# A tiled softmax: ten loads and thirteen stores of mixed sizes become eight and eight of 16 rows per partition, and the last three groups are scaled by one broadcasting VectorE multiplication each

## The chip, the core and the metric

The kernel runs on one core of one Trainium2 chip. The metric is the device time of one execution in microseconds (us). Five engines of the core appear here: DVE (VectorE), ACT (ScalarE), POOL (GpSimd), SP (SyncE, which only issues transfers) and PE (TensorE, not used). Transfers run on 16 DMA engines. The letter q behind an engine's name (ACTq, SPq) means its instruction queue, which issues DMAs and waits on semaphores.

## The reference

The input x has the shape 16 x 1024 x 512 in float32. The output is the softmax over the last axis:

```python
x_max = np.max(x, axis=-1, keepdims=True)
exp_x = np.exp(x - x_max)
return (exp_x / np.sum(exp_x, axis=-1, keepdims=True)).astype(np.float32)
```

There are 16,384 rows of 512 numbers, 2 KB each. Both the input and the output have 33.55 MB, so 67.1 MB pass through the DMA engines in any version.

## The kernel before

**Chunks.** The rows are cut into chunks. A chunk with R rows per partition has 128 x R rows; partition p holds R neighbouring rows, so each partition's piece of a chunk is one contiguous stretch of R x 2 KB in memory. `CHUNKS` lists R and the place in the on-chip buffer `held`, which has room for 96 rows per partition (`SBUF_ROWS`). Before the change there are ten chunks: of 3, 5 and 8 rows, and then seven of 16. The first eight fill the buffer. The last two reuse places: chunk 8 takes rows 0 to 15, where chunks 0, 1 and 2 were, and chunk 9 takes rows 16 to 31, where chunk 3 was.

**Groups.** The work on a chunk is done in groups of at most `GROUP` = 8 rows (lines 108 to 116), 17 groups in all. For each group there are four steps, all in place in `held`:

- `rowmax` (line 127): one DVE reduction gives the negative maximum of each row, `shift`.
- `exps` (line 135): one ACT activation per row computes exp(x - max) and its sum, `sums`.
- `scale`, first part (line 147): one DVE reciprocal of the sums, `recip`.
- `scale`, second part: the rows are multiplied by `recip`. All groups but the last `ON_VECTOR` = 3 do it on POOL, with one tensor_tensor instruction whose second operand is `recip` broadcast along the row (line 150). The last three do it on DVE, with one tensor_scalar instruction per row (line 157).

**Order.** The order is written by hand: each engine executes its instructions in the order of the loop at lines 173 to 183. For each group it is `rowmax(g)`, `exps(g)`, then `scale` of the group before. At the chunks in `FINISH_BEFORE` the group before is scaled first. So a reciprocal usually stands behind the next group's reduction on DVE, and a store stands behind the next group's activations on ACT.

**Loads** (line 122) are issued on SP's queue. The first `EARLY` = 8 are issued at once, three of them ahead of the barrier that opens the program (`AT_HEAD`). The other two stand behind stores (`AFTER_STORE`): load 8 is issued behind store 2's group and must wait until the stores of the places that it overwrites have landed; load 9 likewise waits for both stores of chunk 3.

**Stores** (line 163) are issued on ACT's queue. Each waits for the multiplication of its rows. `STORE_ROWS` lets chunks 3, 4 and 5 be stored in halves of 8 rows, so there are 13 stores: of 3, 5 and 8 rows, six halves of 8 rows, and four of 16 rows. A partition's piece of a transfer appears in the trace as one packet: 6, 10, 16 or 32 KB.

Of the kernel before, what the change touches and what calls it, by code (L numbers as in the profile page):

```python
# [1 line left out]

# [4 lines left out]

F32 = mybir.dt.float32
EXP = mybir.ActivationFunctionType.Exp
AX = mybir.AxisListType.X  # L10


CHUNKS = [
    (3, 0), (5, 3), (8, 8), (16, 16), (16, 32), (16, 48), (16, 64), (16, 80), (16, 0), (16, 16),
]
SBUF_ROWS = 96

EARLY = 8
AFTER_STORE = {2: [8], 3: [9]}

GROUP = 8

FINISH_BEFORE = (1, 2, 3)

STORE_ROWS = {3: 8, 4: 8, 5: 8}

ON_VECTOR = 3

ON_ACT = ()

AT_HEAD = {mybir.EngineType.SP: 3}

def loads_at_the_head(nc):

    main, body = nc.main_func.blocks[0], nc.main_func.blocks[1]
    for engine, count in AT_HEAD.items():
        loads = [
            i  # L40
            for i in body.instructions
            if i.engine == engine and type(i).__name__ == "InstDMACopy"
        ][:count]
        barrier = next(
            n
            for n, i in enumerate(main.instructions)
            if i.engine == engine and type(i).__name__ == "InstDrain"
        )
        for load in loads:
            body.instructions.remove(load)  # L50
        main.instructions[barrier:barrier] = loads


def one_barrier_on_exit(nc):


    end = nc.main_func.blocks[2].instructions

    def of(engine, kind):
        return [i for i in end if i.engine == engine and type(i).__name__ == kind]  # L60

    for engine in (
        mybir.EngineType.Activation,
        mybir.EngineType.PE,
        mybir.EngineType.DVE,
        mybir.EngineType.SP,
    ):
        arrivals = [i for i in of(engine, "InstDrain") if i.has_update()]
        leaves = of(engine, "InstEventSemaphore")
        assert len(arrivals) == len(leaves) == 2  # L70
        end.remove(leaves[0])
        end.remove(arrivals[1])
    gather, release, gather_2, release_2 = of(mybir.EngineType.Pool, "InstEventSemaphore")
    end.remove(release)
    end.remove(gather_2)

@with_exitstack
def kernel(
    ctx: ExitStack,
    tc: tile.TileContext,  # L80
    x: bass.AP,
    out: bass.AP,
):
    nc = tc.nc
    nc.at_finalize(loads_at_the_head)
    nc.at_finalize(one_barrier_on_exit)
    P = nc.NUM_PARTITIONS

    x_flat = x.flatten_outer_dims()
    out_flat = out.flatten_outer_dims()  # L90
    n, d = x_flat.shape
    assert n == P * sum(R for R, _ in CHUNKS)


    src, dst, at = [], [], 0
    for R, _ in CHUNKS:
        for flat, views in ((x_flat, src), (out_flat, dst)):
            part = flat[at : at + P * R, :]
            views.append(part.rearrange("(p r) d -> p r d", r=R))
        at += P * R  # L100

    data = ctx.enter_context(tc.tile_pool(name="data", bufs=1))
    stats = ctx.enter_context(tc.tile_pool(name="stats", bufs=4))
    held = data.tile([P, SBUF_ROWS, d], F32, name="held")
    place = [held[:, s : s + R, :] for R, s in CHUNKS]


    groups = []
    for k, (R, _) in enumerate(CHUNKS):
        m = -(-R // GROUP)  # L110
        cuts = [R * i // m for i in range(m + 1)]
        since = 0
        for a, b in zip(cuts, cuts[1:]):
            ends = b == R or b - since >= STORE_ROWS.get(k, R)
            groups.append((k, a, b, since if ends else None))
            since = b if ends else since
    shift = [None] * len(groups)
    sums = [None] * len(groups)

    def load(k):  # L120
        queue = nc.scalar if k in ON_ACT else nc.sync
        queue.dma_start(out=place[k], in_=src[k])

    def rowmax(g):
        k, a, b, _ = groups[g]
        shift[g] = stats.tile([P, b - a], F32, name="shift", tag="shift")
        nc.vector.reduce_max(  # L127
            out=shift[g], in_=place[k][:, a:b, :], axis=AX, negate=True
        )

    def exps(g):
        k, a, b, _ = groups[g]
        sums[g] = stats.tile([P, b - a], F32, name="sums", tag="sums")
        for r in range(a, b):
            nc.scalar.activation(  # L135
                out=place[k][:, r, :],
                in_=place[k][:, r, :],
                func=EXP,
                bias=shift[g][:, r - a : r - a + 1],
                scale=1.0,  # L140
                accum_out=sums[g][:, r - a : r - a + 1],
            )

    def scale(g):
        k, a, b, since = groups[g]
        recip = stats.tile([P, b - a], F32, name="recip", tag="recip")
        nc.vector.reciprocal(out=recip, in_=sums[g])  # L147
        on_pool = g < len(groups) - ON_VECTOR
        if on_pool:
            nc.gpsimd.tensor_tensor(  # L150
                out=place[k][:, a:b, :],
                in0=place[k][:, a:b, :],
                in1=recip.unsqueeze(2).to_broadcast([P, b - a, d]),
                op=mybir.AluOpType.mult,
            )
        for r in () if on_pool else range(a, b):
            nc.vector.tensor_scalar_mul(  # L157
                out=place[k][:, r, :],
                in0=place[k][:, r, :],
                scalar1=recip[:, r - a : r - a + 1],  # L160
            )
        if since is not None:
            nc.scalar.dma_start(  # L163
                out=dst[k][:, since:b, :], in_=place[k][:, since:b, :]
            )
        if b == CHUNKS[k][0]:
            for later in AFTER_STORE.get(k, ()):
                load(later)

    with tc.manual_schedule():  # L170
        for k in range(EARLY):
            load(k)
        waiting = None
        for g, (k, a, _, _) in enumerate(groups):
            if waiting is not None and a == 0 and k in FINISH_BEFORE:
                scale(waiting)
                waiting = None
            rowmax(g)
            exps(g)
            if waiting is not None:  # L180
                scale(waiting)
            waiting = g
        scale(waiting)


# [1 line left out]
_INS = ['x']  # L187
_OUTS = [((16, 1024, 512), 'float32')]


# [23 lines left out]
```

## Time and profile before

| what | value |
| --- | --- |
| median of four runs | 161.56 us (161.42 to 161.57) |
| the profiled execution's own time | 161.57 us |
| its span, first to last event of the program | 159.7 us |
| DVE busy | 82.6 us (52%) in 58 instructions |
| ACT busy | 92.9 us (58%) in 257 instructions |
| POOL busy | 91.2 us (57%) in 18 instructions |
| DMA, mean over the span | 67.13 MB, 420 GB/s |

The page divides the span into 40 slices and gives for each the busy tenths of every engine and the mean busy share of the 16 DMA engines. A line per DMA queue says how many packets and bytes it moved and what share of 16 engines' time its packets took: q1 carries SP's loads, q10 carries ACT's stores. The groups list the busy time and the mean duration of each instruction form. The timeline gives single instructions with their start, and in brackets what ended the idle time before them. The chain of waits follows back from the last *instruction*; a DMA that lands after it is not part of it. Beside these views the trace holds one record per DMA packet (queue, start, duration, size), and the prediction uses these too.

### The profile page before, as it was taken

What the parts mean: (1) busy time and instruction counts of PE and PEld (TensorE: products, weight loads), DVE (VectorE), ACT (ScalarE), POOL (GpSimd) and SP (SyncE); (2) the same over time, 40 slices, a digit from 0 to 9 for tenths busy, and PEclk for the clock granted to TensorE, in tenths of its full rate; (3) what the DMA queues carried; (4) which work ended last, traced back from release to release, by engine and by line L of the source; (5) the groups of instructions that cost most, each with busy time, mean ns of one, the idle gap of its engine ahead of it and who ended that gap; (6) DMA issues with size and microseconds to landing.
All of it is one profiled execution on the core that took longest, in us unless ns stands there. A gap on an engine that the chain in (4) does not pass through costs nothing.

```text
span 159.7 us, 442 instructions
## 1 busy us (share of the span) xinstructions
DVE 82.6 (52%) x58; ACT 92.9 (58%) x257; POOL 91.2 (57%) x18
## 2 busy tenths in 40 slices
DVE  0470903980966567393855867387489935000000
ACT  0719076039949796976979957993995760000000
POOL 0060912940899999999999999999930000000000
DMA  7999989999999999999999999989999999999993
GB/s 279 431 455 403 438 367 448 476 397 397 460 414 439 418 427 431 460 410 435 418 480 414 412 435 423 480 369 447 431 435 492 396 427 443 443 410 418 484 402 164
DMA packets 3316, 67.13 MB, mean 420 GB/s; under 512 B 369, under 2 KB 369, under 8 KB 625
## 3 DMA queue, kind: packets, MB, share of 16 engines
q1 hardware_dynamic: 1440, 33.56, 49.5%
q10 hardware_dynamic: 1872, 33.56, 48.9%
q14 instruction: 4, 0.02, 0.0%
HBM read 33.55 MB, written 33.55 MB: 420 GB/s over the span
## 4 chain that ended last, share of the span: by engine, by line
POOL 51%; issue 12%; ACT 11%; DVE 7%; DMA 3%; ACTq 0%; DVEq 0%; POOLq 0%
POOL held L150 51%; ACT held L135 11%; DVE held L157 4%; DMA held<-in_x_dram 3%; DVE shift L127 3%; ACTq L163 0%; DVE recip L147 0%; DVEq L209 0%; POOLq L150 0%; DVEq L147 0%; ACTq L135 0%
## 5 line engine op out<-in xcount | busy, mean ns | idle before, releaser
L135 ACT ACTIVATE held<-held,shift 128x512 f32<-128x512 f32 x128 | 90.4, 708 | 33.0 <-POOL held L150 29.9
L150 POOL TENSOR_TENSOR held<-held,recip 128x4096 f32<-128x4096 f32 (+2 forms) x14 | 91.0, 6526 | 25.8 <-DVE recip L147 25.8
L127 DVE TENSOR_REDUCE shift<-held 128x8 f32<-128x4096 f32 (+2 forms) x17 | 70.3, 4139 | 5.3 <-DMA held<-in_x_dram 5.2
L147 DVE RECIPROCAL recip<-sums 128x8 f32<-128x8 f32 (+2 forms) x17 | 3.4, 200 | 46.0 <-ACT held L135 46.0
L135 ACT ACTIVATION_READ_ACCUMULATOR held<-held,shift 128x1 f32 x128 | 23.9, 187 | 0.0
L157 DVE TENSOR_SCALAR held<-held,recip 128x512 f32<-128x512 f32 x24 | 10.0, 489 | 0.1
L135 ACT ACT_TABLE_LOAD x1 | 1.3, 1283 | 4.5 <-DMA held<-in_x_dram 4.5
L198 POOL MEMSET const-float32-0.0<- 128x1 f32 x1 | 0.1, 98 | 0.2 <-issue 0.2
L198 POOL MEMSET const-bfloat16-1.0<- 128x1 bf16 x1 | 0.1, 101 | 0.0
L198 POOL MEMSET const-uint8-127<- 128x1 uint8 x1 | 0.1, 101 | 0.0
L198 POOL MEMSET const-float32-1.0<- 128x1 f32 x1 | 0.1, 98 | 0.0
## 6 DMA issues: line engine op xcount, KB each, us to landing
held<-in_x_dram SPq DMA_DIRECT2D x7, 4096.0 KB, 39.0
out_dram<-held ACTq DMA_DIRECT2D x4, 4096.0 KB, 29.2
out_dram<-held ACTq DMA_DIRECT2D x7, 2048.0 KB, 38.0
held<-in_x_dram SPq DMA_DIRECT2D x1, 2048.0 KB, 11.5
held<-in_x_dram SPq DMA_DIRECT2D x1, 1280.0 KB, 7.1
out_dram<-held ACTq DMA_DIRECT2D x1, 1280.0 KB, 20.5
held<-in_x_dram SPq DMA_DIRECT2D x1, 768.0 KB, 4.4
out_dram<-held ACTq DMA_DIRECT2D x1, 768.0 KB, 15.9
```

What stands on the lines that cost most here:

```text
L127: nc.vector.reduce_max(out=shift[g], in_=place[k][:, a:b, :], axis=AX, negate=True)
L135: nc.scalar.activation(out=place[k][:, r, :], in_=place[k][:, r, :], func=EXP, bias=shift[g][:, r - a : r - a + 1], scale=1.0, accum_out=s ...
L147: nc.vector.reciprocal(out=recip, in_=sums[g])
L150: nc.gpsimd.tensor_tensor(out=place[k][:, a:b, :], in0=place[k][:, a:b, :], in1=recip.unsqueeze(2).to_broadcast([P, b - a, d]), op=mybir.A ...
L157: nc.vector.tensor_scalar_mul(out=place[k][:, r, :], in0=place[k][:, r, :], scalar1=recip[:, r - a : r - a + 1],)
L198: nc = _bacc.Bacc("TRN2", target_bir_lowering=False, num_devices=1)
```

## The change

All chunks now have 16 rows per partition: eight loads and eight stores, each of 4 MB with packets of 32 KB, and 16 groups of 8 rows. Six loads are issued at the start; load 6 follows store 0 and load 7 follows store 1, each into the place that the store has read. No chunk is stored in halves, and no chunk asks for an early `scale`. The last three groups stay on DVE, but each is multiplied by one tensor_tensor instruction with the broadcast reciprocal in place of eight tensor_scalar instructions.

```diff
-CHUNKS = [
-    (3, 0), (5, 3), (8, 8), (16, 16), (16, 32), (16, 48), (16, 64), (16, 80), (16, 0), (16, 16),
-]
+CHUNKS = [(16, 0), (16, 16), (16, 32), (16, 48), (16, 64), (16, 80), (16, 0), (16, 16)]
 SBUF_ROWS = 96
 
-EARLY = 8
-AFTER_STORE = {2: [8], 3: [9]}
+EARLY = 6
+AFTER_STORE = {0: [6], 1: [7]}
 
 GROUP = 8
 
-FINISH_BEFORE = (1, 2, 3)
-
-STORE_ROWS = {3: 8, 4: 8, 5: 8}
+FINISH_BEFORE = ()
+
+STORE_ROWS = {}
 
 ON_VECTOR = 3
...
         nc.vector.reciprocal(out=recip, in_=sums[g])
-        on_pool = g < len(groups) - ON_VECTOR
-        if on_pool:
-            nc.gpsimd.tensor_tensor(
-                out=place[k][:, a:b, :],
-                in0=place[k][:, a:b, :],
-                in1=recip.unsqueeze(2).to_broadcast([P, b - a, d]),
-                op=mybir.AluOpType.mult,
-            )
-        for r in () if on_pool else range(a, b):
-            nc.vector.tensor_scalar_mul(
-                out=place[k][:, r, :],
-                in0=place[k][:, r, :],
-                scalar1=recip[:, r - a : r - a + 1],
-            )
+        engine = nc.gpsimd if g < len(groups) - ON_VECTOR else nc.vector
+        engine.tensor_tensor(
+            out=place[k][:, a:b, :],
+            in0=place[k][:, a:b, :],
+            in1=recip.unsqueeze(2).to_broadcast([P, b - a, d]),
+            op=mybir.AluOpType.mult,
+        )
         if since is not None:
```

## The prediction

> **What bounds the kernel now.** I first read the page's slices and DMA queues. They say that the 16 DMA engines are nine tenths busy or more in 38 of 40 slices, all but the first and the last, and that the two queues' packets take 49.5 + 48.9 = 98.4% of 16 engines' span.
>
> ```profile
> DMA  7999989999999999999999999989999999999993
> ...
> q1 hardware_dynamic: 1440, 33.56, 49.5%
> q10 hardware_dynamic: 1872, 33.56, 48.9%
> ```
>
> The chain of waits names POOL, with 51%. It is misleading here: it starts from the last instruction, and the timeline (DVE and ACT's queue, the last lines) shows that this is the last store's issue at 134.02, some 25 us before the span's end.
>
> ```profile
> 109.16 4.42 DVE L127 TENSOR_REDUCE shift<-held 128x8 f32<-128x4096 f32 x1 [0.75 <-DMA held<-in_x_dram]
> ...
> 120.20 4.40 DVE L127 TENSOR_REDUCE shift<-held 128x8 f32<-128x4096 f32 x1
> ...
> 130.49 0.20 DVE L147 RECIPROCAL recip<-sums 128x8 f32<-128x8 f32 x1 [2.48 <-ACT held L135]
> 130.73 3.26 DVE L157 TENSOR_SCALAR held<-held,recip 128x512 f32<-128x512 f32 x8
> 134.02 0.34 ACTq L163 DMA_DIRECT2D out_dram<-held  x1
> ```
>
> The source view of the store's line, cut to the last store, gives the time from its issue to its landing; the windows of 134 to 158 us show what the core does meanwhile (DVE, ACT and POOL busy, granted clock, DMA share, GB/s).
>
> ```profile
> L163 ACTq DMA_DIRECT2D out_dram<-held x1: 338/338/338, 134.0 to 134.0; - x1
> ...
> DMA to landing us min/median/max: 25.0/25.0/25.0
> ```
>
> ```profile
> 134.00:158.00 24.00, 0.00 (x0) 0.00 (x0) 0.00 (x0) 1.00 0.97 421
> ```
>
> So the last store waits some 14 us behind other stores (its first packet starts at 147.8). The compute engines have that much in hand at the end. The bound is the sum of the packets' durations, and a change moves the time in two ways: other packets, or a stretch in which the queues hold nothing.
>
> **The terms.** All durations are from the profiled execution: time 161.57 us, span 159.74, so 1.83 lies outside; its time is 0.01 over the median of the runs.
>
> 1. *Packets.* The packet records give the mean durations. Loads: 128 packets of 6 KB at 268 ns, 128 of 10 KB at 397, 128 of 16 KB at 614, 896 of 32 KB at 1229. Stores: 128 of 6 KB at 234, 128 of 10 KB at 385, 896 of 16 KB at 611, 512 of 32 KB at 1214. Divided by 16 engines that is 79.05 us for loads and 78.03 for stores, 157.1 in sum. After the change there are 1024 + 1024 packets of 32 KB, 64 + 64 per engine. Stores at 1.214 give 77.7. Loads are bounded by the typical 1.213 (the median) and the mean 1.229, which holds slower packets of 1.25 to 1.55 us before 41 us: 77.6 to 78.7; I take 78.1. The sum is 155.8, **1.3 us less** (bounds 0.7 to 1.8). Nothing else changes in the DMA's work: the first packet comes 0.99 us after the start, as before. With no empty queue the span is 158.4 and the time 160.3.
>
> 2. *A later start of compute.* The first reduction waits for 4 MB in place of 768 KB: 8 packets per engine x 1.213 + 0.99 + 0.3 for slow first packets = 11.0, landed at about 11.8 (the records show 0 to 1 us from the last packet to the landing) in place of 4.4. Then reduction 4.4, eight activations 5.75, reciprocal and waits 0.45: POOL starts at 22.4. Two multiplications take 13.55 to 13.95 together, so store 0 is issued at about 36.2, where before it was 11.5. This costs nothing by itself: six loads are queued from the start and fill the DMA engines until 0.99 + 48 x 1.213 = 59 us even alone. What it moves is the share of the loads, below.
>
> 3. *The two late loads.* Before, store 0's first packet came 3.46 us after its issue (11.53 to 14.99). So it comes at 39.7 now, and runs beside the loads. The packet records show one load packet and one store packet in turn on each engine: loads 5 to 8 landed at 50.9, 65.4, 80.0 and 94.5, every 14.5 us, which is 8 x (1.213 + 0.611). With 32 KB on both sides a round costs 2.427, 19.4 per 4 MB. Store 0 is thus through at 59.1 and landed 1.5 to 2.1 later (as stores 0 to 2 before). Load 6 is issued at 61, and load 5's last packet comes only at about 79: 18 us of cover. Load 7 waits for store 1 (80.5) and is needed at 98: the same cover. Nothing else is queued behind these waits on SP.
>
> 4. *The end.* By 39.7 each engine has moved (39.7 - 1.3) / 1.2135 = 31.7 load packets of 64. The other 32.3 come in rounds of 2.427: the loads end at E = 39.7 + 78.4 = 118.1. By then 32.3 store packets are through, and 56 - 32.3 = 23.7 packets of stores 4 to 6 are left, 28.8 us. Store 7 must reach the engines by **E + 28.8**. On the way to it: landing and wake-up 1.07 (load 9 before: last packet 108.09, reduction 109.16); reduction 4.42; reciprocal 0.15; multiplication of group 13; reduction of group 15, 4.40; eight activations 5.79 with the wait; reciprocal and waits 0.34; multiplication of group 15; issue 0.04. Group 14's multiplication lies beside the 5.79 of the activations. POOL's last multiplication ends at about 118, before group 13's turn, so it isn't late. Without the two multiplications this is 16.2.
>
> The trace has no DVE tensor_tensor. The nearest rows, same page, groups kept apart by shape:
>
> ```profile
> L150 POOL TENSOR_TENSOR held<-held,recip 128x4096 f32<-128x4096 f32 x12 | 83.8, 7014 | 13.1 <-DVE recip L147 13.1
> L127 DVE TENSOR_REDUCE shift<-held 128x8 f32<-128x4096 f32 x15 | 65.7, 4388 | 0.9 <-DMA held<-in_x_dram 0.8
> ...
> L157 DVE TENSOR_SCALAR held<-held,recip 128x512 f32<-128x512 f32 x24 | 10.0, 489 | 0.1
> ```
>
> Below, eight tensor_scalar take 3.26 together (the timeline's x8); above, POOL takes 7.01 for the same operation. I take 4.39, DVE's own reduction over the same 4096 elements: same engine, one instruction, the same shape. The store is then issued at E + 25.0 and, with the 3.46 of term 3, reaches the engines at E + 28.4: 0.4 us in hand. With 3.26 it is E + 26.2 and 2.6 in hand. With 7.01 group 14's multiplication also outlasts the activations by some 1.3, and it is E + 35.0, 6.2 too late. An earlier or later store 0 changes this by its own shift; its latency cancels, since it stands on both sides. Slow packets in the loads' part, up to 0.9 per engine before (the excess of 10 to 50 us), make the loads end later against the stores' rest and take from the 0.4. I book **0.3 us of empty queue**, between 0 and the 0.5 that 0.9 of slow packets would leave.
>
> [...]
>
> 5. *The rest.* Seven fewer transfers save issue time of about 0.34 each on ACT and SP, beside other work: nothing. 24 DVE instructions become three: counted in term 4. Cover gone: the 14 us that the last store had to spare shrink to about 4 from its issue to its turn.
>
> Sum: 161.57 - 1.3 + 0.3 = **160.6 us**.
>
> **The rivals.**
>
> *The last store comes too late (slower).* Place: between E and store 7. Everything that adds to the chain beyond 0.4 us leaves the DMA engines empty, one for one; both multiplications count. It decides against the change from 1.3 + 0.3 of empty queue, that is 2.0 us more on the chain: a multiplication of 5.4 each, or stores that take one packet in twenty more than their half (E is then some 4 later). At 6 us per multiplication the gap is 2.8 and the time 163.1; with the bound 7.01 it is 6.2 and 166.5. For it speaks that the margin is 0.4 and rests on durations from other phases; against it, that DVE's and ACT's rows hardly vary (4.38 to 4.42, 5.75).
>
> *The packet gain is mostly not there (same).* If the 16 ns of excess per load packet have a cause that stays, the saving is 0.7; with 0.5 of empty queue the time is 161.4. For it: 0.9 of the 1.3 us saved comes from the excess of loads over 1213 ns and the small first loads. Against it: the slow packets fall into stretches of 13.7 to 22 and 33 to 35 us only.
>
> *All goes well (more gain).* Loads at 1.213, no empty queue, engines that end together (they ended between 157.5 and 158.7): 159.6.
>
> **How the numbers follow.** Forecast 160.6 (160.1 to 161.1): 0.50. More gain, 159.6: 0.06. Same, 161.4: 0.17. Last store too late, 162 to 165: 0.27. I call 0.2% (0.32 us) what can be told from no change: faster is below 161.24, slower above 161.88. Faster 0.56, same 0.17, slower 0.27. The two likely signs being opposed, the forecast's own range stands above; for 8 in 10 the range reaches into the late store up to a gap of some 2.7 us: 159.8 to 163.0. The bound 166.5 lies outside, since it needs POOL's duration on another engine; I give it 0.03.
>
> **What would show it.** Packets of 32 KB alone, their shares summing to about 155.8 us; load 7 landing near 119; a DVE TENSOR_TENSOR near 4.4 us; last store issued near 143 and landing about 14 to 15 us later (4 of queue, 9.7 of its own packets, the landing). Wrong is the prediction if the DMA share falls below 9 tenths between 120 and 155, if the last store lands within 13 us of its issue (the queue was empty), or if loads and stores share other than packet by packet.

## The result and the profile after

The changed kernel takes 161.81 us (median) against 161.53 us before; the ratio is 1.0019, 95% interval 1.0013 to 1.0026. So it is slower by 0.3 us, at the edge of what can be told apart. Of its 43 executions 41 lie between 161.50 and 162.37 us, and two at 163.66 and 164.19. The profiled execution has 161.86 us and a span of 160.03. The forecast was 160.6 (160.1 to 161.1), with a chance of 0.56 for "faster".

The page of the changed kernel has these lines on the DMA engines: busy tenths and GB/s in 40 slices of 4.0 us, then the queue of the loads (q1) and of the stores (q10) with packets, MB and share of 16 engines' span.

```profile
DMA  7999999999799999999999999999999999999993
GB/s 262 459 459 393 442 475 393 426 467 418 311 461 410 410 475 426 410 467 418 410 459 418 434 426 453 426 410 475 426 410 459 410 426 450 434 426 418 467 426 139
...
q1 hardware_dynamic: 1152, 33.55, 49.6%
q10 hardware_dynamic: 1152, 33.55, 48.6%
```

The engines are as busy as before, and the two shares sum to 98.2% of 160.0 us, 157.1: the same 157 us of packets as before, where 155.8 were forecast. One slice stands out, the eleventh, 40 to 44 us, with 311 GB/s. The windows at the start, around this slice and in the undisturbed end (DVE, ACT, POOL busy, granted clock, DMA share, GB/s) show what kind of loss it is.

```profile
1.00:3.00 2.00, 0.00 (x0) 0.00 (x0) 0.00 (x0) 1.00 1.10 344
...
39.00:42.00 3.00, 0.00 (x0) 3.00 (x9) 3.00 (x1) 1.00 1.10 350
...
118.00:147.00 29.00, 22.45 (x8) 12.80 (x36) 2.10 (x1) 1.00 1.00 432
```

From 39 to 42 the engines are "busy" and yet move 350 GB/s where 432 is usual: packets are in flight for longer. The row of 1 to 3 us has the same mark. The packet records say which. Load packets that begin between 37 and 43 us take up to 2.33 us where 1.213 is usual, 0.98 us too much per engine. Store 0 was issued at 36.7, and its first packet starts at 41.3; loads that begin before that packet have 0.94 of the 0.98. So the loss lies between the store's issue and its first packet, and not beside its packets. The other place is the start: the first load packet of each engine takes 1.5 to 2.3 us, 0.61 too much on average. Outside these two places the loads lose 0.05. In sum the loads' packets take 79.28 us per engine (forecast 78.1) and the stores' 77.72 (forecast 77.7).

The end went as the prediction's steps have it. In the timeline (DVE and ACT's queue):

```profile
120.87 4.42 DVE L125 TENSOR_REDUCE shift<-held 128x8 f32<-128x4096 f32 x1 [8.86 <-DMA held<-in_x_dram]
...
125.43 4.42 DVE L147 TENSOR_TENSOR held<-held,recip 128x4096 f32<-128x4096 f32 x1
...
140.31 4.42 DVE L147 TENSOR_TENSOR held<-held,recip 128x4096 f32<-128x4096 f32 x1
144.82 0.34 ACTq L154 DMA_DIRECT2D out_dram<-held  x1
```

The source view of the last store gives its way to the landing:

```profile
DMA to landing us min/median/max: 14.5/14.5/14.5
```

Before, the last store had 25.0 us from issue to landing; now it has 14.5, and the packet records let it start at 147.82, with no pause behind store 6. So the time in hand shrank as forecast, and the queue did not run dry.

The last of the 16 engines ends at 158.99, the mean of the 16 at 158.00. Before it was 158.69 and 157.83. The 0.3 us between the last ends are the difference between the two profiled executions. The sum of the packets does not explain them, since it fell by 0.08, from 157.08 to 157.00. Three other terms do:

- Neighbouring packets of an engine overlap in the records by some 3 ns, and a sum of durations counts that time twice: 0.58 us per engine before, with 184 packets each, and 0.40 after, with 128. So the sum credits the larger packets with 0.18 us too much.
- The start and small gaps hold 0.07 more than before.
- The last engine ends 0.99 us behind the mean, before it was 0.86: 0.13 more.

Together that is -0.08 + 0.18 + 0.07 + 0.13 = 0.30. It is an account of one execution of each kernel.

### The profile page after: what moved, and what is told of

Read it like the earlier page. It is cut to its first block, busy times and chain, and to the rows that moved or that the text cites. A ratio compares the mean times of both kernels' runs of the same rounds, so it can differ in the third digit from the quotient of the medians.

```text
span 160.0 us, 399 instructions
## 1 busy us (share of the span) xinstructions
DVE 85.5 (53%) x35; ACT 92.7 (58%) x257; POOL 91.0 (57%) x17
## 4 chain that ended last, share of the span: by engine, by line
DMA 51%; POOL 16%; DVE 11%; ACT 7%; issue 4%; DVEq 0%; SPq 0%
DMA held<-in_x_dram 32%; DMA out_dram<-held 19%; POOL held L147 16%; ACT held L133 7%; DVE held L147 6%; DVE shift L125 6%; DVE recip L145 0%; SPq L120 0%; DVEq L145 0%; DVEq L125 0%
## 5 line engine op out<-in xcount | busy, mean ns | idle before, releaser
L147 POOL TENSOR_TENSOR held<-held,recip 128x4096 f32<-128x4096 f32 x13 | 90.8, 7015 | 28.9 <-DVE recip L145 28.9
L125 DVE TENSOR_REDUCE shift<-held 128x8 f32<-128x4096 f32 x16 | 70.2, 4392 | 35.4 <-DMA held<-in_x_dram 35.3
L145 DVE RECIPROCAL recip<-sums 128x8 f32<-128x8 f32 x16 | 3.2, 200 | 23.7 <-ACT held L133 23.7
L147 DVE TENSOR_TENSOR held<-held,recip 128x4096 f32<-128x4096 f32 x3 | 13.3, 4425 | 0.1
```

The costliest lines, as they stand in the source:

```text
L125: nc.vector.reduce_max(out=shift[g], in_=place[k][:, a:b, :], axis=AX, negate=True)
L147: engine.tensor_tensor(out=place[k][:, a:b, :], in0=place[k][:, a:b, :], in1=recip.unsqueeze(2).to_broadcast([P, b - a, d]), op=mybir.AluO ...
```

## The experiments

**Theory A**, formed from the trace after: the time is the sum of the packets plus stretched load packets at the start and where the stores join the loads; the chain behind the last load still has time in hand. **Theory B**: the slower multiplication, twice on the last chain, is what costs. **Rival C**: the stores' equal share makes the last load so late that the queue runs dry. Times are medians; each ratio is to the kernel before, run beside it on the same chip. On the four chips the kernel before has 161.49 to 161.53 us, so times can also be held against the 161.81 of the changed kernel. Readings of packets are from one profiled execution of each kernel.

**The multiplication alone, in the kernel before (e1).**

```diff
-        on_pool = g < len(groups) - ON_VECTOR
...
+        engine = nc.gpsimd if g < len(groups) - ON_VECTOR else nc.vector
+        engine.tensor_tensor(
```

> The kernel before with one thing of the change: one DVE tensor_tensor for each of the last three groups. Theory A (the time is the sum of the packets plus a few stalls of the DMA engines; the chain behind the last load has time in hand): the last store is issued about 2.3 us later than 134.0 and still waits behind other stores, so the time is that of before, 161.5 within 0.2, ratio 0.999 to 1.001. Theory B (the slower multiplications, twice on the last chain, are what the changed kernel pays for): about 0.3 us or more slower, ratio 1.002 or above.

Measured: 161.66 us, ratio 1.0011 (1.0002 to 1.0020). The last store is issued at 136.42, 2.4 us later than before, and its first packet still starts at 147.8:

```profile
136.42 0.34 ACTq L156 DMA_DIRECT2D out_dram<-held  x1
```

The 2.4 us vanish in the queue, as A says. The 0.1% does not lie in the work: the span is 159.6 us against 159.7 before (medians), and on the mean of its 11 executions 2.03 us lie outside the span, where the kernel before has 1.83. The packet records have an 8 KB packet on q14, the instruction queue, at 161.04, after the end of the work; the kernels before and after have none there. That it costs the 0.2 us is not shown.

**The change without the multiplication (e2).**

```diff
-        engine = nc.gpsimd if g < len(groups) - ON_VECTOR else nc.vector
-        engine.tensor_tensor(
...
+        for r in () if on_pool else range(a, b):
+            nc.vector.tensor_scalar_mul(
```

> The changed kernel with the eight tensor_scalar per group back. Theory A: the last store is issued about 2.3 us before 144.8 and its first packet still starts near 147.8, so the time stays 161.8 within 0.2, ratio to before 1.000 to 1.003. Theory B: the time falls back to 161.5 or, if the queue was about to run dry, to the 160.3 of the prediction without a gap.

Measured: 161.73 us, ratio 1.0020 (1.0007 to 1.0033). The last store is issued 1.4 us sooner than in the changed kernel, and its first packet starts at 147.86, no sooner. (It is not 2.3 us sooner, as expected, since load 7 landed 1.0 later, at 121.75.)

```profile
143.41 0.34 ACTq L161 DMA_DIRECT2D out_dram<-held  x1
```

B falls: without the slow multiplication the kernel is as slow.

**Whole stores in the kernel before (e3).**

```diff
-STORE_ROWS = {3: 8, 4: 8, 5: 8}
+STORE_ROWS = {}
```

> The kernel before with chunks 3, 4 and 5 stored whole: 10 stores in place of 13, 32 KB packets in place of 16 KB. Theory A: 48 packets of 611 ns per engine become 24 of 1213, 0.2 us less, and the loads get half of the rounds in place of two thirds, so the last load lands later by several us while the last store keeps some hand; time 161.3, between 161.0 and 161.6. Rival C (equal shares make the last load so late that the queue runs dry): 162 or more, with a DMA share under 9 tenths in the last slices.

Measured: 161.97 us, ratio 1.0025 (1.0015 to 1.0035). Here rival C does happen. The last load lands at 125.5 in place of 109.1, since the loads get half of the rounds and not two thirds; the last store is issued at 147.19, and its first packet starts at 148.04. The windows' row between shows the queue dry for a moment (DMA share 0.69):

```profile
147.00:149.00 2.00, 0.15 (x1) 0.00 (x0) 0.00 (x0) 1.00 0.69 295
```

The expected 161.3 was wrong: the 0.2 us saved on packets are gone (the sum is 157.06, before 157.08), and a first stretch of empty queue is there. It also shows a store that needed only 0.85 us from issue to first packet, where its own queue was just running out.

This kernel also shows a join that cost next to nothing. No store packet is in flight from 53.5 to 58.1 us; then 32 KB stores join the running 32 KB loads again. The loads that begin between 55 and 62 us lose 0.02 us per engine, and the window has no mark (500 GB/s at a share of 1.16 is the same 431 per full share as undisturbed):

```profile
58.00:62.00 4.00, 1.31 (x2) 4.00 (x13) 4.00 (x2) 1.00 1.16 500
```

**One more reduction on the last chain (e7).** Group 15's maximum is computed twice.

```diff
-            rowmax(g)
+            for _ in range(2 if g == len(groups) - 1 else 1):
+                rowmax(g)
```

> The changed kernel with group 15's reduction done twice, 4.4 us more on the chain behind the last load; the output is the same. In the changed kernel the last store was issued at 144.8, 3.0 us before its turn at 147.8. The store is now issued at 149.2. Theory A with a short way from issue to first packet (0.85 us, as the e3 kernel's last store shows): first packet at 150.1, a gap of about 2.2 us in the DMA engines and a time of 164.0. With the 3.46 us of the prediction: gap near 4.9, time 166.7. Rival (the chain never matters): 161.8.

Measured: 163.83 us, ratio 1.0149 (1.0132 to 1.0166). The timeline's last line and the windows' row at the hole:

```profile
150.73 0.34 ACTq L154 DMA_DIRECT2D out_dram<-held  x1
```

```profile
147.00:152.00 5.00, 3.65 (x1) 0.00 (x0) 0.00 (x0) 1.00 0.43 184
```

By the medians the kernel loses 2.0 us. The profiled execution, the slowest of its four (164.42), loses 2.6. In it the store comes 5.9 us later than in the changed kernel (4.4 for the reduction, the rest because load 7 landed 1.6 later). Each engine stands idle for 0.5 to 4.1 us, 2.9 on average, until first packets at 151.6, again 0.85 after the issue. The hole takes up the spread of the engines: they now end between 161.32 and 161.49, where in the changed kernel they end between 157.5 and 159.0. So the mean end is 3.4 us later and the last end, which counts, 2.5. The tail mechanism of the "slower" rival is thus real once the time in hand is used up; in the changed kernel it isn't used up. Its price was less than one for one here: the first packets are 3.8 us later, the last end 2.5.

**Reading early on ACT's queue (e4) and writing early on it (e8).** Both put one small transfer ahead of everything.

```diff
+        warm = data.tile([P, 128], F32, name="warm")
+        nc.scalar.dma_start(out=warm, in_=src[7][:, 0, 0:128])
```

> The changed kernel with one more transfer: ACT's queue first loads 512 B per partition (64 KB in all, into a tile that nothing reads). In the changed kernel each engine loses about 0.9 us to slow load packets between 38 and 42 us, some 3 us after the first store's issue. Theory A1 (it comes with the first use of ACT's queue): the stall moves to the first 5 us, where it may lie partly beside the start, and no slow packets remain near 40; time 0 to 0.8 us less than 161.8, plus 0.1 for the added packets. Rival A2 (it comes with the first packets that write to memory, or with the turn from loads alone to both): slow packets stay near 40 us, time 161.8 to 162.0.

```diff
+        first = data.tile([P, 128], F32, name="first")
+        nc.vector.memset(first, 0.0)
+        nc.scalar.dma_start(out=dst[7][:, 0, 0:128], in_=first)
```

> The changed kernel with one more store ahead of everything on ACT's queue: 512 B per partition of zeros into rows of chunk 7 that the last store overwrites. Reading early on that queue left the stall near 40 us where it was. Theory A2a (the stall comes with the first writes to memory, once): the slow load packets near 40 us are gone, others stand in the first 8 us; time between 161.0 and 162.0. Theory A2b (it comes whenever the stores join a stretch of loads alone): the stall near 40 us stays, and a smaller one may appear at the early store; time 161.9 to 162.2.

Measured: 162.13 us, ratio 1.0041 (1.0027 to 1.0055), and 162.29 us, ratio 1.0047 (1.0034 to 1.0060). The windows of 38 to 42 us, first with the early read, then with the early write:

```profile
38.00:42.00 4.00, 0.57 (x1) 4.00 (x13) 4.00 (x1) 1.00 1.11 377
```

```profile
38.00:42.00 4.00, 0.28 (x1) 4.00 (x12) 4.00 (x1) 1.00 1.05 344
```

Both rows have the mark again, a full DMA share with few GB/s. The stretched packets stay near 40 us, 0.9 to 1.0 us per engine. So it is neither the first use of the queue nor the first write to memory. The small early transfers themselves stretch nothing, although their packets run beside the loads, from 5 to 15 us; they take 0.2 us per engine, part of the 0.3 and 0.5 us that these kernels lose against the changed one. With that both times lie above the ranges given.

**A small first load (e5).**

```diff
+        if k == 0:
+            nc.sync.dma_start(out=place[0][:, 0:1, :], in_=src[0][:, 0:1, :])
+            nc.sync.dma_start(out=place[0][:, 1:16, :], in_=src[0][:, 1:16, :])
+            return
```

`AT_HEAD` goes from 3 to 4 with it, since load 0 is now two transfers.

> The changed kernel with load 0 split in two transfers: 1 row per partition (2 KB packets), then the other 15 rows. Every engine's first load packet took 1.5 to 2.3 us in the changed kernel where 1.213 is usual, 0.60 us of excess per engine; the kernel before began with 6 KB packets and had about 0.25 there. Theory A (the first packet in flight is stretched whatever is asked for, and more when it is large): the excess of the first 2 us falls to 0.3 or less and the time by about 0.3, to 161.5. Rival (a fixed start-up loss): excess and time as in the changed kernel, 161.8.

Measured: 162.28 us, ratio 1.0047 (1.0033 to 1.0061). The expectation of theory A fails. The 2 KB packets lose 0.20 us per engine and the 30 KB packets behind them 0.36, so the first 4 us hold 0.56 us of excess, in the changed kernel 0.63. So the loss at the start is nearly a fixed one, as the rival has it, and the loads' packets still sum to 79.3 us per engine. The time is 0.5 us worse than the changed kernel, which neither side expected. 0.1 of it lies outside the span; the profiled execution, at 161.94 the fastest of this kernel, doesn't show the rest.

**Chunk 0 in halves (e6), and all chunks in halves (e11).**

```diff
-STORE_ROWS = {}
+STORE_ROWS = {0: 8}
```

> The changed kernel with chunk 0 alone stored in halves, so that the first store is issued 7 us earlier, near 29.8, in 16 KB packets. Theory A (the stall belongs to the first store): the slow load packets move from 38 to 42 us to about 31 to 35 and their sum stays near 0.8 to 1 us per engine; the last load lands some 4 us sooner, the last store has that much more in hand, and the time stays at 161.8 within 0.3, since the queue did not run dry anyway. Rival (the stall belongs to the fourth load, which ended just then): slow packets stay near 40 us.

```diff
-STORE_ROWS = {}
+STORE_ROWS = {k: 8 for k in range(8)}
```

> The changed kernel with every chunk stored in two halves of 8 rows: all store packets have 16 KB. Where only chunk 0 was in halves, the stretch at the first store was 0.6 us per engine in place of 0.97, and more followed at 82 and 100 us, when 32 KB stores had begun. If the stretch goes with the size of the store packets: 0.6 us in all after the start, stores' packets 78.2 us (0.5 more), time 161.8 to 162.0. The last load lands some 5 us or more sooner than at 120.8, since loads get two thirds of the rounds. If the stretch comes with loads of 32 KB alone: 0.9 as before, time 162.1 or more.

Measured: 162.13 us, ratio 1.0034 (1.0023 to 1.0046), and 162.28 us, ratio 1.0051 (1.0033 to 1.0069). In both, the stretched packets move to 31 to 40 us with the first store and lose 0.6 us per engine there, less than the 0.98 of the changed kernel with its 32 KB stores. But more comes later: 0.6 at 81 to 104 us in e6, and 0.5 at 94 to 103 in e11 (with 0.2 of the stores), where load 6 landed (89.6) before load 7 was issued (91.3), so the loads joined anew. The loads' sums are 79.6 and 79.5. In e6 I see no such join at 81 to 104; its cause stays open. The last load lands at 119.5 in e6, 1.3 us sooner than in the changed kernel where 4 were expected, and at 111.6 in e11, 9.2 sooner; neither time is better for it. The time of e6 lies just above its range. That of e11 lies where it was expected if the stretch does not go with the size of the store packets.

**The load in flight in halves (e12).**

```diff
+        if k == 3:
+            nc.sync.dma_start(out=place[3][:, 0:8, :], in_=src[3][:, 0:8, :])
+            nc.sync.dma_start(out=place[3][:, 8:16, :], in_=src[3][:, 8:16, :])
+            return
```

> The changed kernel with load 3 alone, the one in flight when the stores join at 38 to 42 us, split in two transfers of 8 rows, so its packets have 16 KB. If the stretch goes with the size of the load packet in flight: about half of 0.97 us per engine near 40. If it is a fixed cost of the join, or goes with the store packet: 0.9 to 1.0 as in the changed kernel. Time 161.5 to 162.0.

Measured: 161.97 us, ratio 1.0029 (1.0018 to 1.0039). The loads lose 0.8 us per engine at 38 to 42, not half of 0.98. In this execution the stretch doesn't go with the size of the load packets in flight.

**The first store later (e9, e10, e14).** Stores 0 and 1 (in e9 store 2 too) are taken out of `scale` and issued behind a later group's activations; loads 6 and 7 follow them. The edit of e10:

```diff
-        if since is not None:
+        if since is not None and k >= 2:
...
+            if g == 6:
+                store(0)
+                store(1)
```

> The changed kernel with the first store held back to about 56 us (behind the activations of group 7), so that loads 0 to 5 run nearly alone to their end near 59.9 and stores 0 to 2 follow; loads 6 and 7 stay behind stores 0 and 1. Theory J (load packets are stretched when stores join a running stream of loads, 0.97 us per engine in the changed kernel): few load packets are stretched near 58 to 62, the loads' packets sum to about 78.4 us per engine in place of 79.3, and the time falls to about 161 if the hand-over leaves no gap, less than before's 161.5; the first store may need 1 to 4 us from issue to first packet, so a gap of up to 1.5 us may eat it. Rival K (the stretch comes with the first large store wherever it stands): stretched packets of either queue near 58 to 72, time 161.8 or more.

> As the kernel with the first store held back to 56 us, but behind the activations of group 6, near 51 us, so that load 5 is still in flight when the stores join. Theory J: stretched load packets near 53 to 57, about 0.9 us per engine, no gap; time 161.8 as the changed kernel. Rival K: the same. The two kernels together tell how much of the time is the join and how much a gap.

> As e10, but stores 0 and 1 stand behind the activations of group 5, so the first is issued some 6 us sooner, near 45, in the middle of load 4. If a later join is better by itself (more of the loads run without it, more time in hand at the end): between e10 and the changed kernel, 161.4 to 161.8. If the join costs the same wherever it stands: packets of the loads near 79.2 us again and a time between 161.4 and 161.9 that follows the engine that ends last.

Measured, with the issue of the first store: e14 (group 5, 46.5 us) 161.85 us, ratio 1.0031 (1.0011 to 1.0050); e10 (group 6, 52.1 us) 161.39 us, ratio 0.9995 (0.9984 to 1.0006); e9 (group 7, 57.7 us) 162.58 us, ratio 1.0064 (1.0049 to 1.0080). The windows in which the stretch now lies, of e14, of e10 and of e9:

```profile
47.00:51.00 4.00, 2.88 (x3) 3.65 (x12) 4.00 (x2) 1.00 0.85 270
```

```profile
52.00:57.00 5.00, 3.85 (x3) 4.25 (x13) 5.00 (x1) 1.00 0.95 354
```

```profile
83.00:87.00 4.00, 2.13 (x2) 4.00 (x13) 4.00 (x2) 1.00 0.99 354
```

The loss moves with the join, to 47 to 50 us and 53 to 57, at 0.9 and 0.7 us per engine. In e9, where load 5 is nearly through when the stores begin, nothing is stretched at that point; but after load 6 has joined the stores (issued at 70.8), stores lose 0.2 at 74 and loads 0.7 at 84 to 85. Neither J nor K has that. Theory J's gain isn't there: the loads' packets sum to 79.2 in all three. In e10 load 6 joins the stores in the same way, at 75, and the loads lose only 0.1 from 70 to 90. What separates e10 from e14 is less the sum than the spread: its engines end between 157.3 and 158.5, those of e14 between 157.6 and 159.1. The trace of e9 is its fastest execution (161.92), so it doesn't show why the median is 162.58. For e10 161.8 was expected; why it is 0.4 us better than the changed kernel is open, beyond its narrower spread.

**e10 with the old multiplication (e13).** The edit of e10 and the edit of e2 together.

> The changed kernel with stores 0 and 1 held back to 52 us, as in e10, and the eight tensor_scalar per group of the kernel before. e10 itself measured 161.39 with its last store issued 8 us ahead of its turn. If the multiplication form has a cost outside the last chain (0.1% in e1 and e2, each with an interval that nearly reaches zero): 161.2 to 161.3, below the kernel before. If those 0.1% are the spread of the engines' ends: 161.4 as e10.

Measured: 161.48 us, ratio 0.9997 (0.9988 to 1.0005). No better than e10. Both take back what the change lost, but neither can be told from the kernel before.

## Why the prediction was wrong, step by step

- **What bounds the kernel** was right. The DMA engines bound the kernels here: with the multiplication alone changed (e1, e2) the time moved by no more than 0.1%. In e7, where the last store came too late for its turn, compute did count.
- **Term 1, packets, failed**, and with it the gain. The sum 155.8 took the loads at 78.1, half way between the typical packet and the mean of before. They came to 79.28, above both bounds given (77.6 to 78.7), and the sum to 157.0: 0.1 us saved where 1.3 were forecast. The excess over 1213 ns was read as slow packets of which half might go. In the changed kernel all of it but 0.05 us lies at two events, and both grew: the first packets of the load stream have 0.61 us per engine, where the first 6 us of the kernel before held 0.37, and the join of stores and loads has 0.98. Before, the join (12 to 22 us) held 0.54, and 0.24 more stood at 32 to 36 us, where no transfer joins. In all kernels run here the sum stays between 156.8 and 157.9 us: smaller first packets, an earlier or a later join and other store sizes moved the excess about and took away 0.2 us of it at most (e10). The stores' durations, 0.3 saved, were right to 0.02, but by the overlaps some 0.1 of these 0.3 was no time.
- **Term 2, the later start**, was right: the first reduction starts at 12.2 (the landing was forecast for 11.8), POOL at 22.7 (22.4), store 0 is issued at 36.7 (36.2), and the load queue held work throughout.
- **Term 3, the late loads**, was right: one load packet and one store packet in turn, load 6 issued at 62.3 and load 7 at 81.6, both long before their turn. The turns change after every 32 KB row piece, which the trace shows as one packet, and each 4 MB of loads 5 to 7 takes 19.4 us.
- **Term 4, the end**: the mechanism was right, with sizes off. E was 119.2 (118.1 forecast, later by the stretched packets), the multiplication 4.42 (4.39), the store's issue E + 25.6 (E + 25.0). The 3.46 us to the first packet were wrong here: that was a store joining a running stream, and the last store, behind its own queue, needed 0.85 in e3 and e7. So this latency does not cancel, as the prediction has it: store 0 took 4.5 and the last one could do with 0.85. So 2.1 us were in hand, not 0.4, and the booked 0.3 of empty queue didn't come.
- **The books**: 160.6 forecast, + 1.2 for the loads' packets, - 0.3 for the gap that didn't come: 161.5, the time before. The remaining 0.3 to 0.4 us is what the sum of durations leaves out: 0.18 of overlaps, 0.13 of a last engine that ends later beside the mean, 0.07 at the start and in small gaps. The prediction carried these over from before unchanged, without saying so.
- **The rivals.** "The packet gain is mostly not there" is what happened, with 0.17 of chance and a price of 161.4; even its 0.7 us of remaining gain were too much. "The last store comes too late" did not decide, but e3 and e7 show it close by. That the time still lies in the wide range of 159.8 to 163.0 is luck: that range was made for a late store, which did not come.

Still open: why the first join stretched packets in flight (by 0.98 us per engine in the changed kernel, 0.9 in e14, 0.7 in e10, 0.6 in e6 and e11), and later joins sometimes did (0.7 in e9, 0.5 in e11) and sometimes didn't (0.02 in e3, 0.1 in e10); and why the start, the overlaps and the last engine's end differ as they do. That these make up the 0.3 us is an account of one execution of each kernel. The halves of the change can't be told apart: e2 has the whole 0.2% without the multiplication, and the 0.1% of e1 lies outside the span.

## What to carry to other kernels

When transfers already fill the DMA engines, look at the packet durations before you credit larger ones: in the kernel before two 16 KB store packets took 1222 ns (twice the mean of 611) and one of 32 KB 1213 (the median), so there was nothing to win on the stores but 0.3 us in 157. Part of that was not even time, because neighbouring packets overlap by some 3 ns in the records of both kernels: check a sum of durations against the engines' last ends. An excess in a mean duration must be placed in time first. If it sits at the start and at the first join, it belongs to events that the new version has too: here they held 0.37 and 0.54 us per engine before, and 0.61 and 0.98 after, with larger packets in flight.

Smaller stores had another use: the engines took turns by packet (beside 16 KB stores 4 MB of loads landed every 14.5 us before, and beside 32 KB stores every 19.4 after), so with 16 KB stores the loads finished sooner (109.1 us before, in place of 125.5 in e3), and that was the time in hand at the end.

## What the runs showed of the hardware

- Where stores of 32 KB first met a running stream of 32 KB loads, load packets in flight took up to 2.3 us in the changed kernel and 2.7 in e2, in place of 1.213: 0.98 us per engine in all in the changed kernel, 0.9 in e14, 0.7 in e10. Using that queue earlier (e4, e8) left it in its place, with 0.9 to 1.0; the two small early transfers showed no such stretch. It was not a price of every join: a later one in e3 cost 0.02.
- Neighbouring packets of an engine overlap by some 3 ns in the records (0.58 us over 184 packets before, 0.40 over 128 after), so the sum of durations overstated the smaller packets, by 0.18 us here.
- The 16 engines ended up to 1.5 us apart in the changed kernel (157.5 to 159.0). In e7 the hole in the queue closed the spread (161.32 to 161.49), so the empty queue cost less there than its length: 2.9 us of it on average moved the last end by 2.5 us and the time by 2.0 to 2.6.
- A store needed 0.85 us from issue to first packet when its own queue was running out (e3, e7), but 3.46 (store 0 before) and 4.5 (store 0 after) when it joined running loads.
